# Buffers that wait only for what lies on their bytes, and four moves around the retention stage

## The chip, the cores and the metric

The kernel runs on one core of one Trainium2 chip. The core has a matrix engine (TensorE, "PE" in the profile), three engines for work on whole tiles (VectorE "DVE", ScalarE "ACT", GpSimd "POOL"), a sync engine ("SP") that mostly starts transfers, and 16 DMA engines that move data between the chip's memory and the on-chip SBUF. Matrix products end in PSUM, eight banks that PE writes and DVE or ACT read. Every engine works through its own list of instructions in order; an instruction waits on semaphores for what it needs, and everything behind it on the same engine waits too. The metric is the device time of one execution in microseconds.

## The reference

The kernel computes one inference step of a decoder with two layers, for 512 prompt tokens and for a sample group of 8 x 4 = 32 tokens that share the weights. Layer 0 mixes by a short gated convolution, layer 1 by retention with 4 heads; a SwiGLU feed-forward follows each. In outline:

```
for layer i in (0, 1):
    x += mixer_i(rmsnorm(x))          # 0: short conv, 1: retention
    x += (silu(h @ w_gate) * (h @ w_up)) @ w_down,   h = rmsnorm(x)
y = rmsnorm(x)

retention: q, k, v, g = split(h @ w_in);  q, k rotated by position, 4 heads
  per chunk of 128 tokens:
    inner = ((q k^T) * decay) v;  cross = (q S) * cross_w
    S = S * chunk_decay + (k * state_w)^T v
  out = (silu(g) * normalised(inner + cross)) @ w_out
```

The model width is 1024, a head has 256 columns of q and k and 512 of v, and the feed-forward is 2816 wide. Outputs are y for both groups, the convolution's last rows and the retention states S.

## The kernel before, in words

**Precision.** Every float32 operand is split into a high part and a low remainder (`split`, L188 on ACT makes the high part, L189 on DVE subtracts), and a product is made of three: high by high, high by low, low by high. Where DVE is short of time the low part is made by `split_adding`: ACT copies the high part (L194), ACT copies it negated (L195), and POOL starts a load that adds the original weights on top (L196). `load_piece` loads a piece of weights on SP's queue (L145) and splits it.

**Stages and pools.** The program runs convolution, feed-forward 0, retention, feed-forward 1, each with its own SBUF pools (`tc.tile_pool`), which are opened in a `with` block and given back at its end, so that the next stage's pools lie on the same bytes. The pools in question are `cv`, `cv1`; `ff`, `ffp`, `sw`, `ffo` of each feed-forward; `rt`, `rt1`, `st` of the retention. As the trace of before shows it, the first load of a new stage (`gt`, L965) goes only when all tiles of the old stage's pools are done, its last write-out (L907) included.

**Feed-forward 0 and what is made ahead.** A job takes two pieces of weights (loaded at L416 and L417, the second one split first), combines them on DVE (L420 to L423) and makes seven block products where the plain way has eight; PE's line is L461, and the operands are combined in the same way (`operand`, L403 to L407). The weights of these jobs use the `sw` pool's `w2`, `h2`, `l2` for the combined piece. At the end of feed-forward 0 the function `ahead` already makes parts of the retention: k and the first half of q of head 0 (L175 by `project`), the values v of head 0 (`value_products`), the second half of q (L175), and then six jobs of gates for heads 0 to 2 (two of the four gates of a head each, `n` = 0 and 2), written to memory with k, q and v (L866, L840, L907).

**Value products.** `value_products` makes a head's v from four weight pieces c = 0 to 3, each 256 rows of the contraction by 512 columns: 24 products a piece (L814 to L816) for the prompt into four PSUM banks, and for the 32 sample tokens eight float32 products (L821) with the unsplit weights, four at a time. Four of them lie in four groups of 32 rows of the output, so that they can run beside each other. `xs` is the sample's input. In the program they stand after pieces 1 and 3; the scheduler may move them.

**Retention, per head.** In heads 0 to 2, PE makes the values of the next head while ACT and DVE prepare this head's operands: `qk_loaded` (L976 load, L979 scale, L1010 to L1015 rotate), `value_loaded` (L1028 `vw`, L1029 `vsw`, L1037 the gates made ahead), `operands_made` (splits of q and k, sample scores L1206, transposed keys L1068, L1077), `value_sample` (L1045) and `sample_operands` (L952, L953). Then come the state products (`mm3`, L163 to L165), the sample's part (L1230, L1232 for outputs, L1248 and DVE's L1253 for the sample states S, loaded at L1222), scores with masks (L1150, L1151), `inner`, the normalisation (L1159 to L1163 and L222, L223), the transposition of the normalised output (L1187) and its product with the gate (L1190, L1194), and the next head's q and k (`qk_project`). `out_project` splits the gated outputs (`yh`, `yl`) and multiplies by the output weights.

PSUM is taken in two ways: `psum()` gives a pair of banks that is read by one instruction, `bank()` a single bank; the pairs rotate among few buffers, so a product into a pair may have to wait for the reader of an earlier one. In `qk_project`, the second k projection has an `inside` and takes single banks; both q projections take pairs.

The last head (h = 3) makes its own four gates within the stage (`gate_project`; L1130 evicts by R, L1131 and L1132 are ACT's silu and scale). `gate_project` with an `inside` runs the first four of eight contraction tiles, then what `inside` issues, then the rest.

**What sets the order.** The program's order gives each engine's list, except that a scheduler may move instructions where data allow; `tc.issue_after(x)` holds what is issued in its block behind instruction x. Semaphore waits are put in by the framework from the tiles' uses.

## Time and profile before

| what | value |
|---|---|
| runs of before | 1486.43, 1489.28, 1489.49 us; median 1489.28 |
| the profiled execution | 1488.64 us, its span 1486.8 us |
| PE busy | 1464.4 us (98%), 10944 records |
| DVE, ACT, POOL busy | 960.4, 611.1, 90.0 us |
| mean granted clock of PE | 0.994 of full |

By stretch of the span, with PE's idle time worked out as the stretch less its busy time:

| stretch, us | stage | PE idle, us | granted clock |
|---|---|---|---|
| 0 to 207 | convolution | 1.2 | 1.00 |
| 207 to 590 | feed-forward 0 | 0.2 | 1.00 |
| 590 to 697 | made ahead for the retention | 1.8 | 0.98 |
| 697 to 1076 | retention, heads 0 to 3 | 11.4 | 0.99 |
| 1076 to 1465 | feed-forward 1 | 0.2 | 1.00 |
| 1465 to 1487 | final norm and last outputs | 7.8 | 0.92 |

How to read the views: a line of the timeline has start, duration, engine, source line, operation, written and read tiles, and in brackets the idle time before it with what ended it. A line of the waits has engine, operation, line, what it waited for, and then total, times and longest in us. A row of the stretches has the stretch, its length, and then busy time with the number of records for PE, PEld (weight loads of PE), DVE, ACT and POOL, the granted clock, the share of the DMA engines and GB/s. PE records overlap, and some are missing, so a busy PE need not be at its best pace.

### The profile page before, as it was taken

To read this page: it belongs to the slowest core of one execution; us is meant where nothing else is said; L and a number is where in the kernel's file an instruction comes from. 1 tells how busy PE (TensorE), PEld (TensorE's weight loads), DVE (VectorE), ACT (ScalarE), POOL (GpSimd) and SP (SyncE) were. 2 spreads that over 40 slices of the span, in tenths; PEclk is the share of its full clock that TensorE was granted. 3 is DMA by queue.
4 is the path that set the end of the run, shared out by engine and by line. 5 is a ranking of instruction groups with operands and counts; after the bars stand their busy time and mean duration, and the time that the engine had idled before them with its cause. 6 is when DMAs were issued, how large, how long until landed. Compare 5 with 4: busy or idle time off the path is not lost.

```text
span 1486.8 us, 26122 instructions
## 1 busy us (share of the span) xinstructions
PE 1464.4 (98%) x10944; PEld 1384.0 (93%) x10944; DVE 960.4 (65%) x1466; ACT 611.1 (41%) x882; POOL 90.0 (6%) x112
## 2 busy tenths in 40 slices
PE   9999999999999999999899999999999999999997
PEld 9999999999999999799489688798799999999997
DVE  6555439848658546774686484595759857748645
ACT  5222355525435335564412322323265624525424
POOL 0000220000000003000000000000030000000002
PEclk9999999999999999999899999999999999999999
DMA  6222273322222316544783673662555232222322
GB/s 223 86 86 86 89 183 100 110 90 95 94 96 97 100 47 156 175 138 145 271 282 131 202 256 103 221 236 84 184 132 124 93 107 86 97 89 100 100 64 82
DMA packets 77446, 194.87 MB, mean 131 GB/s; under 512 B 7168, under 2 KB 24448, under 8 KB 76944
## 3 DMA queue, kind: packets, MB, share of 16 engines
q1 hardware_dynamic: 70272, 172.83, 34.2%
q0 software_dynamic: 2912, 10.56, 4.1%
q10 hardware_dynamic: 4144, 9.81, 1.7%
q8 instruction: 86, 1.41, 0.4%
q14 instruction: 32, 0.26, 0.1%
HBM read 162.29 MB, written 30.88 MB: 130 GB/s over the span
## 4 chain that ended last, share of the span: by engine, by line
PE 92%; DVE 3%; ACT 1%; issue 1%; DMA 1%; POOL 0%; DVEq 0%; SPq 0%; ACTq 0%; POOLq 0%
PE mm L175 36%; PE sm L461 29%; PE sm L175 13%; PE sm L815 2%; PE sm L816 2%; PE sm L814 2%; PE sm L163 2%; PE sm L164 1%; PE sm L165 1%; PE sm L1232 1%; DVE wl L189 1%; PE mm L821 1%; DMA w<-in_rtg_dram 1%; DVE xl L201 1%; PE mm L1248 0%
## 5 line engine op out<-in xcount | busy, mean ns | idle before, releaser
L188 ACT ACTIVATE wh<-w 128x1024 fp32r<-128x1024 f32 (+4 forms) x210 | 204.7, 978 | 393.5 <-PE mm L175 203.7
L189 DVE TENSOR_TENSOR wl<-w,wh 128x1024 fp32r<-128x1024 f32 (+4 forms) x210 | 236.8, 1131 | 42.2 <-ACT wh L188 40.0
L461 PE MATMUL sm<-oh,wh 128*128 128x272 f32 x672 | 194.8, 290 | 1.1 <-ACT wh L188 1.1
L461 PE MATMUL sm<-oh,wl 128*128 128x272 f32 x672 | 194.9, 290 | 0.0
L461 PE MATMUL sm<-ol,wh 128*128 128x272 f32 x672 | 194.5, 289 | 0.0
L175 PE MATMUL mm<-xh,wh 128*128 128x272 f32 x868 | 182.9, 291 | 3.0 <-ACT wh L188 2.8
L175 PE MATMUL mm<-xh,wl 128*128 128x272 f32 x868 | 179.7, 289 | 0.0
L175 PE MATMUL mm<-xl,wh 128*128 128x272 f32 x868 | 179.2, 288 | 0.1
L269 DVE TENSOR_TENSOR x<-x,mm 128x544 f32<-128x544 f32 x85 | 61.2, 720 | 144.7 <-PE mm L175 144.6
L461 PE MATMUL sm<-oh,h 128*128 128x272 f32 x504 | 146.2, 290 | 0.7 <-ACT h L188 0.4
L461 PE MATMUL sm<-oh,l 128*128 128x272 f32 x504 | 146.2, 290 | 0.0
L461 PE MATMUL sm<-ol,h 128*128 128x272 f32 x504 | 145.9, 290 | 0.0
L175 PEld LDWEIGHTS mm<-xh,wh 128*128 128x128 f32 x868 | 135.9, 189 | 5.3 <-ACT wh L188 3.3
L175 PEld LDWEIGHTS mm<-xl,wh 128*128 128x128 f32 x868 | 136.1, 189 | 0.4 <-DVE xl L201 0.3
L175 PEld LDWEIGHTS mm<-xh,wl 128*128 128x128 f32 x868 | 135.5, 189 | 0.6 <-DVE wl L189 0.2
L461 PEld LDWEIGHTS sm<-oh,wh 128*128 128x128 f32 x672 | 127.3, 189 | 2.1 <-ACT wh L188 1.3
L461 PEld LDWEIGHTS sm<-oh,wl 128*128 128x128 f32 x672 | 127.4, 190 | 0.1
L461 PEld LDWEIGHTS sm<-ol,wh 128*128 128x128 f32 x672 | 127.1, 189 | 0.0
L189 DVE TENSOR_TENSOR l<-w,h 128x1024 fp32r<-128x1024 f32 x84 | 80.3, 956 | 57.2 <-ACT h L188 56.9
L175 PE MATMUL mm<-xh,f 128*128 128x272 f32 x576 | 99.3, 288 | 0.0
L461 PEld LDWEIGHTS sm<-oh,h 128*128 128x128 f32 x504 | 95.4, 189 | 1.1 <-ACT h L188 0.7
L461 PEld LDWEIGHTS sm<-oh,l 128*128 128x128 f32 x504 | 95.5, 190 | 0.0
(283 smaller groups left out, 3000.0 us busy)
## 6 DMA issues: line engine op xcount, KB each, us to landing
w<-in_ffgu_dram SPq DMA_DIRECT2D x88, 512.0 KB, 3.5
w<-in_ffdn_dram SPq DMA_DIRECT2D x96, 192.0 KB, 2.5
S<-in_rets_dram SPq DMA_DIRECT2D x16, 1024.0 KB, 7.5
out_rets_dram<-S SPq DMA_DIRECT2D x16, 1024.0 KB, 4.6
w<-in_cvin_dram SPq DMA_DIRECT2D x21, 512.0 KB, 3.4
w<-in_rtqk_dram SPq DMA_DIRECT2D x16, 512.0 KB, 4.4
w<-in_rtv_dram SPq DMA_DIRECT2D x16, 512.0 KB, 3.8
w<-in_rtg_dram SPq DMA_DIRECT2D x16, 512.0 KB, 3.7
```

Of the source, the lines that this page charges most:

```text
L163: nc.tensor.matmul(out, lh, rh, start=start, stop=False, skip_group_check=True)
L164: nc.tensor.matmul(out, lh, rl, start=False, stop=False, skip_group_check=True)
L165: last_product[0] = nc.tensor.matmul(out, ll, rh, start=False, stop=stop, skip_group_check=True)
L175: last_product[0] = nc.tensor.matmul(half(pt, hf)[:, :HT], w[:, c], act[k][:, hf * HT : (hf + 1) * HT], start=(first and k == ks[0] and i ...
L188: h = nc.scalar.activation(dh, src, AF.Copy)
L189: nc.vector.tensor_sub(dl, src, dh.bitcast(F32))
L201: nc.vector.scalar_tensor_tensor(xl[kt][:, c], x[kt][:, c], gain, xh[kt][:, c].bitcast(F32), op0=ALU.mult, op1=ALU.subtract)
L269: last_residual[0] = nc.vector.tensor_add(xk, xk, p)
L461: nc.tensor.matmul(out, w[:, c], b[k][:, at, :], start=(first and k == 0 and i == 0), stop=(k == n - 1 and i == 2), skip_group_check=True,)
L814: nc.tensor.matmul(out, xh[kt][:, ts_], wh[:, cw], start=(kt == 0), stop=False)
L815: nc.tensor.matmul(out, xh[kt][:, ts_], wl[:, cw], start=False, stop=False)
L816: nc.tensor.matmul(out, xl[kt][:, ts_], wh[:, cw], start=False, stop=(kt == KT - 1))
```

## The change

The tile pools of the three kinds of stages get `reuse_waits="tile"`: a new tile waits only for those old tiles that lie on its bytes. Beside it:

- `value_products` issues the sample's products after pieces 1 and 2 (pieces 0 and 1, and 2 and 3), each four held behind the last product of the piece, and asks for pieces c + 2 before the products of piece c.
- In `ahead`, the first v piece of head 0 goes through the `sw` pool (`w2`, `h2`, `l2`) instead of the common weight buffers.
- Both gate tiles of the last head made ahead (h = 2) come from the `fp` pool with tag `f`, not only the second.
- `qk_project` takes single banks whenever `dt` is 1, so now for the second q projection too (before only where `inside` was given: the second k).
- In the last head, `operands_made` goes into the middle of gate 0, gate 1 is issued after `first_outputs`, and `yns` is normalised behind the eviction of gate 3 (`st["scaled"]`).

Line numbers after the first edit are one to five higher in the new kernel (L821 becomes L824, L1187 L1192).

```diff
-        tp = c2.enter_context(tc.tile_pool(name="rt", bufs=2))
-        one = c2.enter_context(tc.tile_pool(name="rt1", bufs=1))
-        sp = c2.enter_context(tc.tile_pool(name="st", bufs=3))
+        tp = c2.enter_context(tc.tile_pool(name="rt", bufs=2, reuse_waits="tile"))
+        one = c2.enter_context(tc.tile_pool(name="rt1", bufs=1, reuse_waits="tile"))
+        sp = c2.enter_context(tc.tile_pool(name="st", bufs=3, reuse_waits="tile"))
...
-            ws = [value_piece(h, c, raw, first is None) for c in range(2)]
+            ws = [value_piece(h, c, raw, first is None, sw=None if c else sw) for c in range(2)]
...
             wh, wl = ws[c]
+            if c < 2:
+                ws.append(value_piece(h, c + 2, raw, first is None and c == 0, after=after if c == 0 else None))
...
-            if c % 2:
-                for g in range(4):
-                    kt = 2 * c - 2 + g
...
-                        start=(c == 1), stop=(c == 3), skip_group_check=True,
-                    )
-            if c < 2:
-                ws.append(value_piece(h, c + 2, raw, first is None and c == 0, after=after if c == 0 else None))
+            if c in (1, 2):
+                with tc.issue_after(last.ins):
+                    for g in range(4):
+                        kt = 4 * (c - 1) + g
...
+                            start=(c == 1), stop=(c == 2), skip_group_check=True,
+                        )
...
-        pv, pvs = value_products(0, xs, then=operand_of)
+        pv, pvs = value_products(0, xs, then=operand_of, sw=sw)
...
-                    last = h == AHEAD - 1 and n
+                    last = h == AHEAD - 1
...
-            pt = [bank(), bank()] if inside else psum()
+            pt = [bank(), bank()] if dt else psum()
...
-            each(lambda p, gi, r: nc.vector.tensor_mul(gi, p, r), pt, g, R)
+            def scaled(p, gi, r):
+                st["scaled"] = nc.vector.tensor_mul(gi, p, r)
+            each(scaled, pt, g, R)
...
-                gate_project(h, st, 0, ws=gw)
-                operands_made(h, st)
-                gate_project(h, st, 1)
+                gate_project(h, st, 0, lambda: operands_made(h, st), gw)
                 value_sample(h, st)
...
                 first_outputs(h, st)
+                gate_project(h, st, 1)
                 state(h, st, 1)
...
-                yns = normalized(st["po"], "rot1")
+                with tc.issue_after(st["scaled"].ins):
+                    yns = normalized(st["po"], "rot1")
```

The pools of the convolution and of the feed-forward get the same argument.

More of the change, by code (lines that the diff above doesn't have):

```diff
@@ L275, in hybrid_decode_kernel @@
     with ExitStack() as c0:
-        tp = c0.enter_context(tc.tile_pool(name="cv", bufs=2))
-        one = c0.enter_context(tc.tile_pool(name="cv1", bufs=1))
+        tp = c0.enter_context(tc.tile_pool(name="cv", bufs=2, reuse_waits="tile"))
+        one = c0.enter_context(tc.tile_pool(name="cv1", bufs=1, reuse_waits="tile"))
         fs = one.tile([P, KT, NB, 6], F32, tag="fs", name="fs")
@@ L540, in ffn @@
         with ExitStack() as c1:
-            tp = c1.enter_context(tc.tile_pool(name=f"ff{layer}", bufs=4))
-            fp = c1.enter_context(tc.tile_pool(name=f"ffp{layer}", bufs=2))
-            sw = c1.enter_context(tc.tile_pool(name=f"sw{layer}", bufs=1))
-            one = c1.enter_context(tc.tile_pool(name=f"ffo{layer}", bufs=1))
+            tp = c1.enter_context(tc.tile_pool(name=f"ff{layer}", bufs=4, reuse_waits="tile"))
+            fp = c1.enter_context(tc.tile_pool(name=f"ffp{layer}", bufs=2, reuse_waits="tile"))
+            sw = c1.enter_context(tc.tile_pool(name=f"sw{layer}", bufs=1, reuse_waits="tile"))
+            one = c1.enter_context(tc.tile_pool(name=f"ffo{layer}", bufs=1, reuse_waits="tile"))
             oh, ol = operand_tiles(one)
@@ L792, in hybrid_decode_kernel, with value_piece, value_products @@
     gate_made = [dram.tile([P, 4, T], F32, tag=f"g{h}", name=nm("gm")) for h in range(AHEAD)]
-    def value_piece(h, c, raw, adding=False, after=None):
-        return load_piece(a["rtv"][h, c], 2 * DV, keep=raw, adding=adding, after=after)
-    def value_products(h, xs, first=None, then=None, ws=None):
+    def value_piece(h, c, raw, adding=False, after=None, sw=None):
+        return load_piece(a["rtv"][h, c], 2 * DV, keep=raw, adding=adding, after=after, sw=sw)
+    def value_products(h, xs, first=None, then=None, ws=None, sw=None):
         pv = [bank() for _ in range(4)]
@@ L815, in value_products @@
                     nc.tensor.matmul(out, xh[kt][:, ts_], wl[:, cw], start=False, stop=False)
-                    nc.tensor.matmul(out, xl[kt][:, ts_], wh[:, cw], start=False, stop=(kt == KT - 1))
-            if c % 2:
-                for g in range(4):
-                    kt = 2 * c - 2 + g
-                    nc.tensor.matmul(
-                        pvs[g * NS : (g + 1) * NS, 0, :], xs[:, kt, :],
-                        raw[kt // 2][:, kt % 2 * DV : (kt % 2 + 1) * DV],
-                        start=(c == 1), stop=(c == 3), skip_group_check=True,
-                    )
-            if c < 2:
-                ws.append(value_piece(h, c + 2, raw, first is None and c == 0, after=after if c == 0 else None))
+                    last = nc.tensor.matmul(out, xl[kt][:, ts_], wh[:, cw], start=False, stop=(kt == KT - 1))
+            if c in (1, 2):
+                with tc.issue_after(last.ins):
+                    for g in range(4):
+                        kt = 4 * (c - 1) + g
+                        nc.tensor.matmul(
+                            pvs[g * NS : (g + 1) * NS, 0, :], xs[:, kt, :],
+                            raw[kt // 2][:, kt % 2 * DV : (kt % 2 + 1) * DV],
+                            start=(c == 1), stop=(c == 2), skip_group_check=True,
+                        )
             if then is not None:
```

## The prediction

> **What bounds the kernel now.** The first part of the page comes first: TensorE (PE) is busy for 1464.4 of the span's 1486.8 us. The change leaves the number of PE products as it is, so only three things can be won: the 22.4 us in which PE stands idle, products that run at half clock, and products that stand badly grouped.

> ```profile
> PE 1464.4 (98%) x10944; PEld 1384.0 (93%) x10944; DVE 960.4 (65%) x1466; ACT 611.1 (41%) x882; POOL 90.0 (6%) x112
> ```

> Then the waits of PE, which name the places:

> ```profile
> PE mm L821 <- DMA w<-in_rtv_dram: 5.2, 1, 5.2
> PE mm L175 <- ACT wh L188: 2.8, 3, 0.9
> ...
> PE sm L163 <- ACT knh L188: 0.9, 1, 0.9
> PE mm L1068 <- DVE gate L1130: 0.6, 1, 0.6
> ```

> Then busy time by stretch of the span (engine columns, then PEclk, the granted clock, 1.00 or 0.50):

> ```profile
> 630.11:633.53 3.42, 3.42 (x17) 3.42 (x17) 3.25 (x5) 1.21 (x3) 0.00 (x0) 0.50 0.59 200
> ...
> 712.03:722.27 10.24, 9.47 (x19) 4.17 (x20) 10.24 (x17) 4.66 (x6) 0.00 (x0) 0.50 0.87 319
> 707.11:712.33 5.22, 0.01 (x2) 0.03 (x1) 5.22 (x8) 1.88 (x2) 0.00 (x0) 0.97 1.04 397
> 719.22:722.27 3.05, 3.05 (x7) 2.50 (x8) 3.05 (x8) 0.96 (x2) 0.00 (x0) 0.50 0.82 328
> 625.00:629.20 4.20, 2.64 (x20) 2.20 (x19) 4.20 (x8) 2.62 (x4) 0.00 (x0) 1.00 0.76 297
> ```

> A "busy" PE of 9.47 us with 19 records is PE waiting for weights at half clock. The reader sees two bad places, 625 to 634 (end of the first feed-forward stage) and 707 to 722 (start of the retention stage). Last, the timelines of SP, DVE, ACT and POOL (start, duration, engine, line; in brackets the idle time before):

> ```profile
> 614.78 0.87 POOL L196 DMA_DIRECT2D wl<-in_rtqk_dram  x1 [15.57 <-ACT wl L195]
> ...
> 620.95 0.33 SPq L417 DMA_DIRECT2D w<-in_rtg_dram  x1
> ...
> 700.39 0.33 SPq L965 DMA_DIRECT2D gt<-in_gtab_dram  x1
> ...
> 701.71 0.49 SPq L1028 DMA_DIRECT2D vw<-vm  x1
> ...
> 705.52 1.29 DVE L979 TENSOR_TENSOR rot<-rot,gt 128x1088 f32<-128x1088 f32 x1 [7.61 <-issue]
> ...
> 710.45 2.00 ACT L188 ACTIVATE vh<-vw 128x1024 fp32r<-128x1024 f32 x2 [12.86 <-DMA vw<-vm]
> ...
> 780.02 0.68 DVE L1190 TENSOR_TENSOR gate<-gate,mm 128x512 f32<-128x512 f32 x1
> ```

> DVE stands idle for 7.6 us and then works without a break until `wl` (717.95, 1.22) is done at 719.17. That chain, not one load, ends last at 719.22, when the products with the low parts (L815) go on.

> **The change, part by part.** Paces by the PE timeline at full clock: a 128x272 product 0.1245 us, a 128x512 one 0.2335. The sample's four value products (L821) lie in four row groups, run together and cost 0.98 us as a group; one alone costs 0.98 too.

> *1. End of the first feed-forward stage (595 to 634).* Before, L821 ran as four, one alone at 614.03 (0.98 us) and three at 619.88 (0.99). After, four follow the second weight piece and four the third: one 0.98 us group goes and a switch (about 0.1) with it, so −1.1, and the projection of the second q starts near 619.75 instead of 620.87. But this projection needs its low weights `wl`, which POOL's adding load brings: issued 614.78, about 6.0 to landing (row of that load in this stretch), so 620.8, and its first use, the fifth product, was due at 621.47. After, ACT has one operand split (1.34) between `wh` and `wl`; the raw weights leave some 0.5 earlier, since the load ahead of them is gone. I get issue at 615.3, landing at 621.2, need at 620.35: a stall of 0.8, so −0.3 is left of 1.1 (ends −1.1 with no stall, +0.4 with the split's full delay). The stalls behind it: the gate's second piece (SP L417, 620.95) waited for the last L821; it now waits for the group at the end of the third piece, about 614.1. It landed at 624.55 and would land near 618, so the gate's weights are ready long before PE asks at 627. PE idled 1.3 (from 626.82) and 0.6 (from 628.47) there: −1.9. In the next 3.41 us the clock was half: some 14 products at 0.227 instead of 0.1245 (the trace lacks a few records), 3.42/2, or −1.7. If the idle goes, this should go. The first v piece now comes through the buffers of the feed-forward weights, during its last jobs: SP issues it behind the `l` split that ends at 535.4, 3.8 to landing, 539.2; ACT reaches its two copies (1.04 and 1.06) at about 543.5 in idle 2.54 us wide (542.7 to 545.23), POOL its load at 545.7, 14 us before its first addition at 559.94. Cost 0; ACT and POOL idle cover it. Sum of the place: −3.9; from −1.5 (the `wl` stall takes 1.5, and its idle halves the clock again) to −4.7.

> *2. Pools that wait by tile, start of retention.* Before, SP's first load (`gt`, 700.39) waited until everything of the feed-forward pools was done, the last gate's write-out (697.62) included; `gt`, both `rot`, `vw` (1024 KB) and more queue behind each other at 397 GB/s. After, `gt` and `rot` wait only for early gates, whose write-outs left at 667.38 and 677.95; they land about 685. `vw` still lies on the last gate's bytes, so it goes at 700.4 instead of 701.71, now with 1.6 MB less ahead of it. The page's median for it is 5.3 to landing: 705.7 instead of 710.45. DVE then does, from 697.95, `rot` 1 (1.29), six rotation steps (3.85) and `rot` 0 (1.28), to 704.4, all in what was idle; after `vw`: ACT's first half, 706.75, `vl` 1.13, six steps 3.85, `vl` 1.13, `wl` 1.13, so 714.0 against 719.17. ACT (`vh` 2.0, `qkh` 1.0, `wh` 1.05) is ready at 709.8. L815 moves by −5.1. PE still idles from 707.1 to about 714, so I keep the half clock; it cost 3.05/2, 1.5, after the restart. How the 3.41 us stretches fall is chance: 3.05 to 6.4 us of half clock after the restart, so 1.5 to 3.2; I take 2.0, +0.5. SP's queue holds nothing urgent behind `vw` but S and the last w, which gain. Place: −4.6; from −1.0 (`vw` takes its old 8.7, landing 709.1, `wl` at 717.4, and the longer half clock) to −6.6 (the clock stays full). The places of the last gates (the h=2 pair in the other pool) decide these waits and cost nothing themselves.

> *3. Head 0, rest.* The state products and L1248 stand as in later heads; the same stretch took 19.85 us in head 0 and 19.34 in head 1: −0.4 (0 to −0.5).

> *4. Second q projection in single banks, heads 0 to 2.* By the waits it is ACT's `wh` (0.9 three times), but that copy ends by accident at the same time. In program order the projection reuses the bank pair of the gated product, read by L1190 (780.02 to 780.70); PE goes on at 780.84. With single banks it needs banks free since 772.4. PE waited 0.92: −2.76. Price: DVE evicts in two instructions (2x0.44, not 0.72), +0.16, off the path: `yl` 3 is ready at 786.3, PE wants it near 787.5. From −1.8 (one head finds another wait) to −2.8.

> *5. Last head.* Gate 0 is split around the operands, in banks: the wait of L1068 (0.57) and the one for `knh` (0.85) lie under the gate's second half: −1.4. New: ACT has silu, a `mid` copy and the gate's scale (0.66+0.57+0.75) ahead of `v2`, +0.3; gate 1's projection stands behind the state update, and waits for DVE's first L1253 (1.2 long, begun 0.54 after L1248), while five products (1.2) and L1248 (0.44) cover 1.7: +0.1; DVE's eviction and weight split of gate 1 (0.72+1.23) come before the scores' mask, +0.2. The end (1068 to 1077) holds 2.6 of waits; the later normalisation lets the gate's eviction go 1.1 earlier, but then `yns` itself comes at 1073.4 instead of 1069.5 and four transposes wait for it: 0. Sum −0.8; from −1.6 to +1.0.

> **Sum.** −3.9 −4.6 −0.4 −2.8 −0.8 = −12.5. The profiled execution took 1488.64 (span and 1.84 around it), 0.64 under the median of the runs: 1476.1 from the one, 1476.8 from the other; I say 1476.5. All good ends together give −16.2 (1472.4), all bad ones −2.8 (1485.9).

> **Rivals.** (a) The retention border keeps its time: `vw` still waits for the last gate, so the chain ends as late as before or the half clock eats the rest; for it, the 8.7 us that `vw` took; against it, the 1.6 MB that no longer stand ahead. Gain 8 to 9: 1480.5. (b) The late `wl` of the second q eats the first place: stall 1.5, half clock again. Gain about 10: 1479. [...] (d) Nothing: the early loads only move and PE waits for something else each time, 1488. (e) Slower: the first v piece's adding load stands on POOL ahead of the six additions of squares (559.94 to 575.85), which feed the norm that PE meets at 585. POOL has 5.7 us of gaps among them; if ACT's two copies wait for a late piece, every us beyond 565.6 costs PE one. To end slower overall the load must be held to about 581, 35 us later than I put it; at 584, 1491.

> **Chances.** Forecast 0.52, (a) 0.17, (b) 0.14, (c) 0.07, (d) 0.04, (e) and what else makes it slower 0.06. A measurement tells about 0.2%, 3 us, from no change. Faster is the forecast with (a) to (c): 0.90; same 0.04; slower 0.06. The range reaches over (a), (b) and (c) and leaves out (d), (e) and the worst sums: 1471 to 1483.

> **What would show it.** Right: no half clock near 630, the adding load before the second q landing at about 621, PE idle under 1 us there; `gt` issued about 20 us before `vw`; DVE busy from 698; low products resuming 7 us, not 12, after the first pieces end; no wait of L175 for `wh` in heads 0 to 2; no wait for `knh`. Wrong: `vw` landing over 8 us after its issue, half clock longer than 6 us after the restart, a wait of PE for POOL's `wl` over 1 us, or a new wait for S or `yns` in the last head over 1 us.

## The result and the profile after

The changed kernel takes 1478.97 us (median of 6 runs, 1478.13 to 1479.31), the kernel before in the same comparison 1489.38 us (6 runs, 1486.43 to 1491.5). The ratio is 0.993, with a 95% interval of 0.9918 to 0.9943: 10.4 us, or 0.7%, faster. The forecast was 1476.5 us in a range of 1471 to 1483. The sign and the range held; the middle was 2.5 us too good, and what happened is close to rival (b), which said 1479.

The profiled execution took 1478.13 us, with a span of 1475.8 us. The first part of the page, one line for the kernel after:

```profile
PE 1458.5 (99%) x10944; PEld 1382.9 (94%) x10944; DVE 959.6 (65%) x1470; ACT 610.5 (41%) x882; POOL 90.1 (6%) x112
```

The count of products is the same, and PE's idle time fell from 22.4 to 17.3 us. The waits of PE (engine, tile, line <- who was waited for: us in total, times, longest):

```profile
PE mm L175 <- DMA wl<-in_rtqk_dram: 2.4, 1, 2.4
PE sm L816 <- ACT wh L188: 2.3, 1, 2.3
PE sm L817 <- DVE wl L189: 2.0, 1, 2.0
...
PE sm L1192 <- DVE yn L1168: 0.6, 1, 0.6
PE mm L1211 <- DVE rot L1015: 0.5, 1, 0.5
PE mm L175 <- ACT yh L188: 0.5, 1, 0.5
```

Three things of the prediction can be read here at once. The wait for the third v piece, 5.2 us before, is now one of 2.3 and one of 2.0. The three waits of the second q projection (L175 for ACT's `wh`, 2.8 us together) are gone, and so are the two ahead of the last head's scores. But at the top stands a wait that was not there before: the second q projection waits 2.4 us for POOL's adding load.

The two traces side by side, by landmarks on PE, show where the time went (start of one product to start of another, us; together −10.5, and the last 0.5 of the span's 11.0 lie behind the last product; below, the second row is called the first place, the third the border, and the points themselves the marks):

| from, to | before | after | difference | forecast |
|---|---|---|---|---|
| start to first V product (L814, now L816) | 595.01 | 595.66 | +0.65 | 0 |
| to head 1's first V product | 96.69 | 95.69 | −1.00 | −3.9 |
| to head 0's first product of the sample's scores with its values (L1230, now L1235) | 46.73 | 41.53 | −5.20 | −4.6 |
| to the same of head 1 | 103.42 | 102.12 | −1.30 | −0.4 −0.92 |
| to the same of head 2 | 103.13 | 102.13 | −1.00 | −0.92 |
| to the first L461 of the last feed-forward stage | 205.59 | 202.66 | −2.93 | −0.92 −0.8 |
| to the last product | 328.69 | 328.95 | +0.26 | 0 |

The first row lies in stages whose code on PE did not move. The +0.65 is in place by the first 30 us. The kernels of the experiments stand between −0.16 and +0.92 there, the lowest with the changed pools in these stages, the highest with the old ones; so it is taken as the scatter of an execution's start.

The border, the start of the retention stage, is the largest gain, and its chain came out close to the forecast. The timeline of the kernel after (start, duration, engine and line; in brackets the idle time before):

```profile
677.89 0.38 SPq L966 DMA_DIRECT2D gt<-in_gtab_dram  x1
683.63 0.80 SPq L977 DMA_DIRECT2D rot<-qkm  x2
700.03 0.38 SPq L1029 DMA_DIRECT2D vw<-vm  x1
```

```profile
697.48 1.27 DVE L980 TENSOR_TENSOR rot<-rot,gt 128x1088 f32<-128x1088 f32 x1
...
705.06 2.01 ACT L188 ACTIVATE vh<-vw 128x1024 fp32r<-128x1024 f32 x2 [7.84 <-DMA vw<-vm]
...
712.24 1.22 DVE L189 TENSOR_TENSOR wl<-w,wh 128x1024 fp32r<-128x1024 f32 x1
...
713.51 0.80 PE L817 MATMUL sm<-wl,xh 128*128 128x512 f32 x1 [1.96 <-DVE wl L189]
```

`gt` leaves 22 us ahead of `vw`, which lands in 5.0 us; DVE's rotations begin at 697.5 in time that was idle, and the low products go on at 713.5. The forecast had 20, 5.3, 698 and 714.0. The clock was half there once more. Busy time by stretch (engine columns, granted clock, DMA share, GB/s):

```profile
621.36:624.77 3.41, 1.22 (x9) 1.22 (x10) 3.22 (x5) 2.47 (x5) 0.00 (x0) 1.00 0.75 223
624.77:628.18 3.41, 3.41 (x18) 3.41 (x17) 1.05 (x2) 2.71 (x4) 0.00 (x0) 0.50 0.78 238
706.70:710.11 3.41, 1.16 (x8) 0.67 (x4) 3.41 (x6) 2.26 (x3) 0.00 (x0) 1.00 1.00 370
710.11:716.94 6.83, 4.13 (x13) 3.12 (x13) 6.83 (x12) 2.34 (x3) 0.00 (x0) 0.50 1.00 362
```

The last two lines are the border: 6.83 us at half clock in place of 10.24, of which 3.43 lie behind the restart of the low products at 713.51. The first two are the end of the first feed-forward stage: the wait for the adding load, and then a full 3.41 us at half clock, just as long as before the change. Three lines of that place explain the wait. The first is POOL's issue of the load, and the second, from another answer, ends with its time from issue to landing in us; both are of the kernel after. The third, in a block of its own, is the same answer before:

```profile
615.18 0.88 POOL L196 DMA_DIRECT2D wl<-in_rtqk_dram  x1 [23.57 <-ACT wl L195]
...
wl<-in_rtqk_dram POOLq DMA_DIRECT2D x1, 512.0 KB, 8.3
```

```profile
wl<-in_rtqk_dram POOLq DMA_DIRECT2D x1, 512.0 KB, 6.0
```

The issue came when the prediction said (615.3). The landing took 8.3 us and not the 6.0 of before. What else was under way is on SP's queue:

```profile
612.75 0.33 SPq L416 DMA_DIRECT2D w<-in_rtg_dram  x1
614.85 0.33 SPq L417 DMA_DIRECT2D w<-in_rtg_dram  x1
615.28 0.37 SPq L416 DMA_DIRECT2D w<-in_rtg_dram  x1
```

Two loads of 512 KB for the first gate now leave at 614.85 and 615.28, around the adding load's issue. Before, the same two left at 620.95 and 621.45, when it had landed.

### The profile page after: what moved, and what is told of

It is laid out like the page before. It is cut to its first block, busy times and chain, and to the rows that moved or that the text cites. A ratio compares the mean times of both kernels' runs of the same rounds, so it can differ in the third digit from the quotient of the medians.

```text
span 1475.8 us, 26100 instructions
## 1 busy us (share of the span) xinstructions
PE 1458.5 (99%) x10944; PEld 1382.9 (94%) x10944; DVE 959.6 (65%) x1470; ACT 610.5 (41%) x882; POOL 90.1 (6%) x112
## 4 chain that ended last, share of the span: by engine, by line
PE 94%; DVE 3%; DMA 1%; issue 1%; ACT 1%; POOL 0%; DVEq 0%; POOLq 0%; ACTq 0%; SPq 0%
PE mm L175 35%; PE sm L461 30%; PE sm L175 15%; PE sm L817 2%; PE sm L818 2%; PE sm L163 2%; PE sm L816 2%; PE sm L1237 1%; PE sm L164 1%; PE sm L165 1%; DVE wl L189 1%; DMA wl<-in_rtqk_dram 1%; PE mm L1253 0%; DVE xl L201 0%; PE mm L1192 0%
## 5 line engine op out<-in xcount | busy, mean ns | idle before, releaser
L188 ACT ACTIVATE wh<-w 128x1024 fp32r<-128x1024 f32 (+4 forms) x210 | 204.5, 977 | 382.8 <-PE mm L175 185.7
L461 PE MATMUL sm<-oh,wh 128*128 128x272 f32 x672 | 194.5, 289 | 0.0
L461 PE MATMUL sm<-oh,wl 128*128 128x272 f32 x672 | 194.2, 289 | 0.0
L461 PE MATMUL sm<-ol,wh 128*128 128x272 f32 x672 | 194.0, 289 | 0.0
L175 PE MATMUL mm<-xh,wh 128*128 128x272 f32 x804 | 170.1, 292 | 0.2
L175 PE MATMUL mm<-xh,wl 128*128 128x272 f32 x804 | 167.0, 290 | 2.4 <-DMA wl<-in_rtqk_dram 2.4
L175 PE MATMUL mm<-xl,wh 128*128 128x272 f32 x804 | 166.8, 289 | 0.0
L461 PE MATMUL sm<-oh,l 128*128 128x272 f32 x504 | 145.6, 289 | 0.0
L461 PE MATMUL sm<-ol,h 128*128 128x272 f32 x504 | 145.4, 289 | 0.0
L461 PE MATMUL sm<-oh,h 128*128 128x272 f32 x504 | 145.3, 289 | 0.0
L175 PEld LDWEIGHTS mm<-xh,wl 128*128 128x128 f32 x804 | 126.1, 190 | 3.2 <-DMA wl<-in_rtqk_dram 2.6
L175 PEld LDWEIGHTS mm<-xh,wh 128*128 128x128 f32 x804 | 126.7, 190 | 1.7 <-ACT wh L188 0.5
L461 PEld LDWEIGHTS sm<-oh,wh 128*128 128x128 f32 x672 | 126.8, 189 | 1.1 <-ACT u L518 0.6
L175 PEld LDWEIGHTS mm<-xl,wh 128*128 128x128 f32 x804 | 127.0, 190 | 0.1
L461 PEld LDWEIGHTS sm<-oh,wl 128*128 128x128 f32 x672 | 126.8, 189 | 0.0
L461 PEld LDWEIGHTS sm<-ol,wh 128*128 128x128 f32 x672 | 126.6, 188 | 0.0
L175 PE MATMUL sm<-xh,wh 128*128 128x272 f32 x476 | 101.6, 291 | 0.0
L175 PE MATMUL sm<-xh,wl 128*128 128x272 f32 x476 | 99.8, 288 | 0.0
L175 PE MATMUL sm<-xl,wh 128*128 128x272 f32 x476 | 99.5, 287 | 0.0
```

Of the source, the lines that this page charges most:

```text
L175: last_product[0] = nc.tensor.matmul(half(pt, hf)[:, :HT], w[:, c], act[k][:, hf * HT : (hf + 1) * HT], start=(first and k == ks[0] and i ...
L188: h = nc.scalar.activation(dh, src, AF.Copy)
L461: nc.tensor.matmul(out, w[:, c], b[k][:, at, :], start=(first and k == 0 and i == 0), stop=(k == n - 1 and i == 2), skip_group_check=True,)
```

## The experiments

Two theories stand for the first place, where 3.9 us were forecast and 1.0 came. Theory: the adding load is late because the gate's loads, freed by the earlier products, run beside it; that stall and the half clock behind it are the whole miss. Rival: the place is limited by something else (gate weights, the copies on ACT), and the stall only stands in front of it. For the rest the question is which edit gave what, since the pools and the five edits beside them came at once. The places of the last gates (h = 2) were not undone by themselves.

### The second q's piece loaded plainly

```diff
-        qw = load_piece(a["rtqk"][0, 1], KT * P, adding=True)
+        qw = load_piece(a["rtqk"][0, 1], KT * P)
```

The low part is now made by DVE, without POOL's load.

> The changed kernel, but the weights of the second q projection made ahead get their low part from DVE instead of from POOL's adding load. Theory (the late landing): in the changed kernel PE waited 2.42 us for that load, and its clock was half for the 3.41 us after; without the load both go, 2.4 + 1.7 = 4.1 less than 1479.0: about 1475, and no half clock between 600 and 690. Rival (the place is bound by what DVE and ACT prepare for the first gate, and the load only stood in front of it): PE waits as long at the first L461, and the time stays within 1 us of 1479.

1475.98 us (4 runs, 1475.53 to 1477.3), ratio 0.9913 (0.9899 to 0.9926); the changed kernel's median lies 3.0 us higher. The waits of PE begin with

```profile
PE sm L816 <- ACT wh L188: 2.3, 1, 2.3
PE sm L817 <- DVE wl L189: 2.0, 1, 2.0
```

so the wait for the adding load is gone; nothing between 600 and 640 us runs at half clock:

```profile
600.00:640.00 40.00, 39.15 (x236) 32.52 (x235) 33.30 (x48) 19.82 (x26) 0.00 (x0) 1.00 0.46 151
```

From the first V product to the gates' first product (L461) the stretch is 31.09 us, against 35.00 in the changed kernel: −3.9. But to head 1's first V product only −2.0 are left. The stretch of the gates is 1.9 us longer instead; part of that is in waits of the gates' products (L461) that the stall had covered: 0.4 for ACT's `h`, 0.3 for DVE's gate, 0.2 for `wl`. So the theory holds for the stall, and the rival for a part of what it hid. By the profiles the place is then worth 2.99 us against before, not the 3.9 of the prediction.

### The gate's loads held back

The adding load is left as it is; a small write-out of `va` goes to SP behind the sample's products, and the first gate's loads are queued behind it, so that they leave at 619.6 to 620.8.

```diff
+        hold = nc.sync.dma_start(held, va[0][:, 0, :32])
...
+        with tc.issue_after(hold.ins) if hold is not None else ExitStack():
+            jobs[0].prepare()
...
+        run(jobs, inside, lambda i: None, hold)
```

> The changed kernel, but the two loads of the first gate's weights queue behind a small write-out of the first v tile (an extra 16 KB transfer), so they leave near 620 instead of 612.75 and 614.85. Theory (contention: two pieces of 512 KB share the DMA engines with the adding load, which took 8.3 us instead of 6.0): the adding load lands in 6.0 to 6.5 us and PE's wait for it falls from 2.4 to under 1 us; in its place PE waits about 2 us at the first L461 for weights that land near 624; sum 1478 to 1481. Rival (the adding load is slow for another reason, such as its place on POOL or what lies in its buffer): it still takes about 8 us, PE waits 2.4 us for it and for the gate's weights too: 1481 to 1483.

1478.46 us (5 runs, 1477.52 to 1479.45), ratio 0.9927 (0.9913 to 0.9941), which is the changed kernel's time. The profile separates what the time does not. The load of the disputed row now lands in

```profile
wl<-in_rtqk_dram POOLq DMA_DIRECT2D x1, 512.0 KB, 5.7
```

PE does not wait for it, and the first L461 comes 4.1 us sooner after the first V product (30.89 against 35.00). Then the gate's weights are late, as before the change:

```profile
PE sm L461 <- ACT gate L519: 0.8, 1, 0.8
PE sm L461 <- DVE wl L189: 0.7, 1, 0.7
```

and 0.46 us are left at head 1's first V product. This shows both halves. The two gate loads beside it are the cause of the late load: the same load took 8.3 us in the changed kernel, where they (L417, L416) leave at 614.85 and 615.28, 5.7 us here, where they leave at 620.25 and 620.80, and 6.0 us in the kernel before, where they leave at 620.95 and 621.45. In these two arrangements one of the transfers is late, and either costs PE about the same.

### The old waits of the pools, everything else changed

```diff
-        tp = c2.enter_context(tc.tile_pool(name="rt", bufs=2, reuse_waits="tile"))
+        tp = c2.enter_context(tc.tile_pool(name="rt", bufs=2))
...
```

and the same for all pools of the convolution, the feed-forward and the retention.

> The changed kernel with all pools waiting as before; the order of all instructions is the same. Theory (the gain at the start of retention, 5.2 us in the profiles, comes from the waits of the pools alone): 1479.0 + 5.2 = about 1484, the first load of the stage again after the last gate's write-out, DVE idle for 7 us there. Rival (the new order of the value products or the new places of the last gates bring it): within 1.5 us of 1479.

1482.47 us (5 runs, 1481.45 to 1482.77), ratio 0.9953 (0.994 to 0.9965): 3.5 us of the gain gone. The border is as long as it was before any change, 47.06 us (46.73 before, 41.53 changed), and its wait is back:

```profile
PE sm L816 <- ACT wh L188: 6.5, 1, 6.5
PE mm L175 <- DMA wl<-in_rtqk_dram: 2.5, 1, 2.5
```

That the time rose by 3.5 us and not by 5.5 is seen at the first place: PE waits 2.5 us for the adding load there too, but in this execution the clock stayed full behind it, and the place is 1.5 us shorter than in the changed kernel (94.20 against 95.69). This is taken up below.

### The new waits on the three retention pools alone

This is the kernel before with `reuse_waits="tile"` on `rt`, `rt1` and `st`, and nothing else.

> The kernel before, with the new waits on the three SBUF pools of the retention stage (rt, rt1, st) and on nothing else: order, banks, gates and the first v's buffers stay as before. Theory: the 5.2 us that the border gave are the restart of head 1's v operands, which these pools held back; the kernel before had its low products of the third v piece at 719.2 and the changed one at 713.5, and with the old waits in the changed kernel that place was 5.4 us longer. So this alone should bring 1489.2 - 5.4 = 1483.8 us, the wait of head 1's third v piece for its high half should fall from some 6.5 to some 2.5 us, and the marks of the later heads should all stand 5 to 5.5 us earlier by one constant. Rival: the border needs the sample's new order or the first v piece's own buffers as well, or another tile's wait takes over; then at most 1 to 2 us come, 1487 to 1488.

1483.91 us (6 runs, 1482.08 to 1488.06), ratio 0.9962 (0.9948 to 0.9977): 6.0 us faster than the kernel before. The border takes 41.59 us, as in the changed kernel. One argument on three pools is enough for the whole border; the sample's order, the first v's buffers and the places of the gates are not needed for it. The pools of the convolution and the feed-forward were not changed alone, so what they give is not shown. The wait for the third piece's high half in this trace is 0.7 us, less than expected, since the old order has the sample's products at that place, which wait themselves. The marks of heads 0 to 2 stand 4.6 us earlier throughout, but the last head of this execution lost 1.3 us again to a half clock that the kernel before does not show there:

```profile
1018.56:1021.97 3.41, 2.17 (x16) 1.45 (x15) 2.13 (x4) 3.38 (x5) 0.00 (x0) 1.00 0.13 10
1021.97:1025.38 3.41, 3.21 (x11) 2.60 (x12) 2.33 (x3) 1.12 (x4) 0.00 (x0) 0.50 0.40 144
```

### The old order of the sample's v, the first v in the common buffers

```diff
-            if c in (1, 2):
+            if c % 2:
...
-        pv, pvs = value_products(0, xs, then=operand_of, sw=sw)
+        pv, pvs = value_products(0, xs, then=operand_of)
```

> The changed kernel with the sample's v as before (its products after the second and fourth v piece, the fourth piece loaded after the products in program order) and head 0's first v piece in the common buffers; pools, banks and last head stay changed. Theory: between the second q projection and head 1's first V product the changed kernel gained only 1.0 us, which this undoes (+1.0), and at the border the sample's products stand in the old place, where they fill none of the 2.3 us wait for the third piece (+0 to 0.5, the products cost the same wherever they stand): 1479.0 + 1.0 to 1.5 = 1480 to 1480.5. Rival: the order of the sample's products matters for the restart of the border, which then loses up to the 5 us it gave: 1484. Another: nothing, 1479.

1478.27 us (5 runs, 1476.04 to 1479.36), ratio 0.992 (0.9906 to 0.9934): no difference from the changed kernel by the medians, a miss for the theory that these edits gave 1 us or more. In the trace the wait for the adding load is gone and the gate's wait of old stands in its place,

```profile
PE sm L461 <- ACT wh L188: 2.0, 1, 2.0
```

with half clock again, as in both other kernels (mean granted clock 0.96 from 600 to 640 us in all three). The border takes 41.68 us. So these edits moved a wait of 2 us from the gates to the second q projection. What that is worth stays open. The profiled execution (1479.31 us) has a first place 1.45 us longer than the changed kernel's (97.14 against 95.69), as the theory said, and the median shows nothing. The clock differs among the executions too: its mean was 0.996 to 0.999 of full here and 0.994 to 0.995 in the changed kernel's runs. The order of the sample's products and the first v's buffers were undone together, so their shares are not separated.

### A bank pair for the second q

```diff
-            pt = [bank(), bank()] if dt else psum()
+            pt = [bank(), bank()] if inside else psum()
```

> The changed kernel, but the second q projection of heads 1 to 3 takes a pair of banks again. Theory (PE waited there for DVE's L1190 to read the earlier pair): 3 x 0.92 = 2.8 more than 1479.0, about 1481.8, with three waits of 0.9 back. Rival (it was ACT's split of weights, as the list of waits says): no change, 1479.

1481.51 us (5 runs, 1479.28 to 1482.9), ratio 0.9946 (0.9934 to 0.9958): 2.5 us slower than the changed kernel, with

```profile
PE mm L175 <- ACT wh L188: 3.3, 4, 0.9
```

back among the waits. By the profile each of the three heads is 1.15 us longer (103.27 and 103.28 against 102.12 and 102.13, and 203.77 against 202.66 for the last mark); the runs spread over 3.6 us. The wait is not for ACT's copy: in the changed kernel the projection of head 0 starts at 773.89, and the copy that the trace names here runs there from 773.90 to 774.96. The wait goes when the projection no longer needs the bank pair that the gated product is read from.

### The last head: its old order, and its norm alone

The first kernel undoes all of the last head's order, the second only the hold of the two outputs' norms.

```diff
-                gate_project(h, st, 0, lambda: operands_made(h, st), gw)
+                gate_project(h, st, 0, ws=gw)
+                operands_made(h, st)
+                gate_project(h, st, 1)
...
-                with tc.issue_after(st["scaled"].ins):
-                    yns = normalized(st["po"], "rot1")
+                yns = normalized(st["po"], "rot1")
```

> The changed kernel with the last head in the old order: both gates one after the other ahead of the scores, and the two outputs' norms not held behind the last scaling. Theory (from the two profiles, where the last head and what follows it is 1.9 us shorter after, beside its single banks): 1479.0 + 1.9 = 1480.9. Rival (the sum of the prediction, 0.8 for this step): 1479.8. A third: the gain came with the pools and not with the order, then 1479.0, no change. In the profile the split should show as 1.2 us between gate 0's first product and the first score, and 0.6 from the scores to the first output product.

> The changed kernel with one edit undone: the last head's two outputs are normalised as soon as they are there, and not behind the last scaling. The prediction put this edit at 0. From the profiles the stretch from the first score to the first output product is 0.65 us shorter in the changed kernel (31.47 against 32.12 us). If the held norms are what gives it, that stretch reads 32.1 here and the time is 1479.0 + 0.6 = 1479.6 us; if it comes with the gates' split, the stretch stays at 31.5 and the time at 1479.0; if the held norms cost something, it is 30.5 to 31 and 1478.2.

The old order took 1479.93 us (5 runs, 1479.27 to 1481.78; ratio 0.9937, 0.9924 to 0.9949), the norm not held 1480.68 (6 runs, 1478.81 to 1482.22; ratio 0.9942, 0.9927 to 0.9957). Against the changed kernel's 0.993 these are 1.0 and 1.8 us, neither clear of the intervals; the profiles tell more. From head 2's scores to the first product of the output projection (L175 for `yh`) there are 128.52 us in the old order, 127.20 with the split alone, and 126.68 in the changed kernel: the split of the gates gives 1.3 and the held norm 0.5. It does so because the eviction of the last gate goes first on DVE. Without the hold DVE starts it at 1058.76 instead of 1057.87, which is 1.2 us later counted from head 2's mark, and PE waits

```profile
PE mm L175 <- ACT yh L188: 1.2, 1, 1.2
```

where the changed kernel waits 0.5 for `yh` and 0.6 for `yn`. In the execution without the hold, the clock was then half for 3.41 us, behind a stretch with 1.39 us of idle time (that wait and what stood around it), which cost 1.2 us more:

```profile
1062.86:1066.27 3.41, 2.02 (x13) 1.57 (x13) 2.92 (x9) 1.39 (x4) 0.72 (x1) 1.00 0.14 53
1066.27:1069.68 3.41, 3.41 (x17) 3.41 (x17) 1.25 (x4) 0.53 (x2) 0.00 (x0) 0.50 0.00 0
```

### Products for nothing, to keep the clock up

The first experiment's kernel, with 8 spare products in each of the border's two waits, into a half of a bank that nobody reads.

```diff
+            if spare and c == 2:
+                with tc.issue_after(last_sample.ins):
+                    for _ in range(8):
+                        last_spare = nc.tensor.matmul(pvs[:, 1, :], xh[0][:, :P], ws[1][0][:, :DV], start=True, stop=True, skip_group_check=True)
...
+                    with tc.issue_after(high.ins):
+                        for _ in range(8):
+                            high = nc.tensor.matmul(pvs[:, 1, :], xh[0][:, :P], wh[:, :DV], start=True, stop=True, skip_group_check=True)
```

> The first experiment's kernel (the second q projection's piece loaded plainly) with 16 products more, for nothing, into a half of the sample's bank whose value is not used by then: 8 right after the sample's first four in head 1's v, where TensorE waits 2.3 us for the third piece's high half, and 8 after that piece's first four high products, where it waits 2.0 us for the low half. Each takes some 0.235 us at the full clock, 1.9 us a group, so they fit the two waits. Theory: the clock halved at 708 because a window of 3.4 us was over half idle; with products in the gaps it stays at full speed, and the 3.4 us at half clock give back 1.5 to 1.7 us: 1476.0 - 1.6 = 1474.4, with no stretch of half clock between 600 and 1400 us. Rival: the waits themselves are what cost, the halved clock lies beside the wait for the low half; then no change (1476.0), or up to 0.6 us slower where the products run past the end of the waits.

1474.18 us (4 runs, 1473.89 to 1476.63), ratio 0.9898 (0.9885 to 0.9912): 1.8 us under the first experiment's kernel by the medians, the fastest of all the kernels here, and 4.8 us under the changed kernel. In the first experiment's kernel PE is busy for 1.10 us of the 3.41 from 704.63 to 708.04, and the clock is half from there to 714.87. Here the border took 40.13 us against 41.59, −1.46, and the granted clock stays full in it:

```profile
690.00:735.00 45.00, 44.07 (x217) 30.85 (x217) 29.08 (x55) 19.47 (x28) 0.34 (x2) 1.00 0.64 237
```

So the waits themselves were not the whole price. The products at half speed behind the two waits were another 1.5 us here, and work that computes nothing removes that part.

## Why the prediction was right and wrong

*1, end of the first feed-forward stage (−3.9; measured −1.00).* This is where it was wrong, and the failing term is one duration: "about 6.0 to landing" for the adding load. It was read from the row of before, where a single gate load, sent 1.4 us ahead of it, ran beside it. The same paragraph moved the gate's loads from 621 to about 614 and counted their gain, and never asked what they would meet there. The landing took 8.3, the stall was 2.4 and not 0.8, and with it the half clock stayed. The idle time of the gates (1.9 us before) did go, and so did the lone product group (1.1); −1.1 −1.9 +2.4 makes −0.6, and 0.4 us of the measured −1.00 stay unassigned. Rival (b) said this: a stall (1.5 us in its sum), the half clock again, 1479. The 5.7 and 8.3 us with the gate loads held and free are the proof; the plain load shows that the step as meant would have given about 3.0, the rest coming back as waits of the gates' products.

The first v piece through the other buffers cost nothing, as said: POOL issued its load at 546.9 (forecast 545.7), 13.7 us ahead of its first addition.

*2, border (−4.6; measured −5.20).* Right in its mechanism and, to within 0.7 us, in the times of the chain from `vw` on, and shown twice, by undoing the pools (+5.5 in that stretch) and by making them alone (−5.1). The half clock behind the restart lasted 3.43 us, 1.7 us lost where 2.0 were put in. Rival (a) fell: `vw` landed in 5.0 us.

*3, head 0's rest (−0.4).* Head 0 gained 0.3 more than head 1 did.

*4, single banks (−2.76).* 0.92 a head was forecast, 1.00 is read at head 2, and undone it costs 1.15 a head; 2.5 us in the medians. It was right to read the wait by program order and banks and not by the engine that the trace named.

*5, last head (−0.8; measured about −1.9).* The direction was right and the size too small. The split gave 1.3 net where −1.4 and +0.6 made 0.8; of the new waits some 0.3 is found at `v2` and at most 0.1 at gate 1, and nothing of the 0.2 at the scores, so what it saved is nearer 1.7 than 1.4, and 0.3 of that is not assigned to a wait. The end, put at 0, gave 0.5, because the hold lets DVE evict the last gate first, and what the norm loses (0.6 of waiting for `yn`) costs less than what the gate gains.

*The clock.* The clock did not stay full at the border (the good end of step 2), and the forecast had said so: it was half for 6.83 us, behind 3.41 us with 2.25 us of idle time. At the first place it was half for 3.41 us behind a stretch with 2.19 us of idle time, and without the norm's hold behind one with 1.39 us.

By the sum, as measured: −1.00 −5.20 −0.3 −3.0 −1.9 makes −11.4, against −12.5 forecast; with +0.65 at the start and +0.26 at the end, −10.5, where the medians differ by 10.4. That the middle was only 2.5 us off is in part luck: the first place brought 2.9 us too little, and the border and the last head 1.7 more than forecast. One sum of the prediction is wrong: its bad ends add up to −3.3, not −2.8. The range leaves them out either way.

## What to carry to other kernels

When a change lets a transfer start earlier, look up which transfer on the path is in flight at the new time, and price that one again: a landing read before the move was measured beside the old neighbours (6.0 us here, and 8.3 beside the new ones). An idle stretch on the bounding engine had two prices here, the wait and the half-clock products after it, and at the border the second (1.5 us) could be avoided alone, by spare products in the gap. Where a stage border stands still for some us, look first at what the first loads of the new stage wait for; here waits by tile on three pools gave half of the whole gain.

## What the runs showed of the hardware

| kernel | stretch, us | PE idle in it, us | granted clock just behind it |
|---|---|---|---|
| before | 626.70 to 630.11 | 1.56 | 0.50 |
| before | 705.21 to 708.62 | 1.50 | 1.00 |
| before | 708.62 to 712.03 | 3.41 | 0.50 |
| changed | 621.36 to 624.77 | 2.19 | 0.50 |
| changed | 706.70 to 710.11 | 2.25 | 0.50 |
| changed | 1061.68 to 1065.09 | 1.26 | 1.00 |
| second q's piece loaded plainly | 704.63 to 708.04 | 2.31 | 0.50 |
| old pools | 618.35 to 621.76 | 1.03 | 1.00 |
| old pools | 621.76 to 625.17 | 1.46 | 1.00 |
| old pools | 703.68 to 707.10 | 2.22 | 0.50 |
| retention pools alone | 1018.56 to 1021.97 | 1.24 | 0.50 |
| norm not held | 1062.86 to 1066.27 | 1.39 | 0.50 |

Idle time in such a stretch alone does not decide: behind 1.24 us the clock was half from 1021.97, while behind 1.46 us (621.76, old pools) and 1.50 us (705.21, before) it stayed full. What else counts stays open. With the old pools the 2.5 us wait at the first place lay across two of these stretches, and the clock stayed full:

```profile
618.35:621.76 3.41, 2.38 (x13) 1.79 (x11) 3.09 (x6) 3.34 (x5) 0.00 (x0) 1.00 1.02 246
621.76:625.17 3.41, 1.95 (x15) 1.95 (x16) 3.05 (x4) 2.12 (x5) 0.00 (x0) 1.00 0.51 178
```

In the changed kernel most of the 2.4 us wait lay in one (621.36, 2.19 us idle), and the clock was half behind it. That the place of the wait among the stretches made this difference is the author's reading; no run moved it alone. At the border the half clock differs among executions too: from 690 to 735 us the mean granted clock was 0.92 in the changed kernel, but 0.89 in the profiles with the bank pair and with the last head in its old order, whose edits lie behind the border. That is 0.03 of 45 us, by estimate 1.4 us of full clock. An edit that is worth as little, as the last head's was, is better read from its stretch of the trace than from the medians.
